# Regrouping a state-space mixer's input and output through DRAM instead of with TensorE transposes

## The chip, the cores and the metric

The kernel runs on one core of a Trainium2 chip. The metric is the device time of one execution in microseconds (us). The engines are called PE (TensorE; PEld is its weight load), DVE (VectorE), ACT (ScalarE), POOL (GpSimd) and SP (SyncE, which only issues DMAs here).

## The reference

A decoder trunk of two layers works on 512 tokens of width 1024, all in float32. In each layer the input is RMS-normalised, one projection makes ten slices of 512 columns, four mixers run on them, each result is multiplied by `silu` of its gate slice, and the output projection is added to the residual. The part that matters here is mixer A, the diagonal complex state-space mixer, run on the slice `u`:

```
h    = rms_norm(x, norm_g);  proj = h @ w_in           # (512, 5120), ten slices of 512
u    = proj[:, 0:512] as (512 tokens, 32 groups, 16)
bu   = einsum('lgh,gph->lgp', u, bbar)                 # complex, 64 states per group
x_l  = abar * x_{l-1} + bu_l                           # scan over the tokens
y    = Re(einsum('lgp,ghp->lgh', x, c)) + d * u
y    = gelu(y.reshape(512, 512))
ga, gb = split(y @ w_glu, 2);  y_a = ga * sigmoid(gb)
mixed = concat(y_a*silu(a_g), y_b*silu(b_g), y_c*silu(c_g), y_m*silu(m_g))
x    = x + mixed @ w_out
```

The other mixers are differential attention (q, k, v), a gated linear recurrence after a width-4 convolution (`cx`; "lru" in the code), and attention into 256 memory tokens.

## The kernel before, in words

Every large product is made of three float32r matmuls: operands are split into a high part and a remainder (`whi`, `wlo` for weights, `hThi`, `hTlo` for the transposed activations). Weights arrive in pieces of 128x1024 (SP's queue), ACT makes `whi` (L166), DVE makes `wlo` (L172), and `w_use` asks for the split of the piece that lies two ahead of the one it hands out. A piece feeds 24 matmuls with 512 moving columns.

`ORDER` lists the projection blocks in the order in which they are run. A block is either token-major (`tm_block`, L537: the activations are the loaded operand and the weights move, result = tokens on partitions) or column-major (`cm_block`, L517: the weights are loaded and the activations move, result = columns on partitions). A block of 512 columns yields eight times, once every 12 matmuls; each yield is a tick. At every tick a small planner (`Streams`) lets each live side stream issue its next portion, and a stream says how many ticks it wants to wait (`D_S5`, `D_AT`, `D_MEM`). So the side streams (attention, lru, memory attention, state-space) are interleaved with the projection matmuls on all engines. `st.join("s5")` ahead of `gl`, the GLU block, issues ticks without projection work until the state-space stream is done.

The state-space stream `s5` works on `U`: partition = (group parity, position within a chunk of four tokens, channel), then 16 group pairs, then 128 chunks. Before the change `u` comes from a token-major block whose loaded operand is `hT` read with a step of four elements (`h_au`), is copied to `au` (L924), and 16 PE transposes with four ACT copies turn it into `U` (L934, L935), one portion of four at each of four ticks. Then, for f = 0 to 3: `states(f)` multiplies `U` by `WT` into the one PSUM tile of tag `sc` (L1004); `turned`, `scans`, `turned_back` are DVE work; `w_rows` and `c_weights` build the weights on DVE, `w_turn` transposes them on PE; `kernel_rows` writes `MT` with eight POOL DMAs (L982); `outputs(f-1)` multiplies `U` by `MT` and `xp` by `VV` (L1010, L1012) with `U` and `xp` as the loaded operands, and ACT copies the result into `yg` (L1014). At the end 16 more PE transposes (L1095) turn `yg`, ACT applies GELU out of PSUM (L1097), and ACT and DVE split the result into `yhi` and `ylo` for `gl`.

Tiles come from pools with a fixed number of buffers: `b8` has 14 of 8 KB, `b2` has ten of 2 KB, PSUM tag `tp` has two banks (shared by all transposes, `outputs`, lru and the memory attention), `sc` one tile of two banks (shared by `states` and the scores of both attentions).

Of the kernel before, what the change touches and what calls it, by code (L numbers as in the profile page):

```python
# [27 lines left out]
ROPE_THETA = 500000.0  # L28


ORDER = ["q v k kv cx au cg bg mq ag mg gl oAM0 oAM1 oBC0 oBC1".split(),
         "q k cx v kv au mq bg mg ag cg gl oAM0 oAM1 oBC0 oBC1".split()]

C_ID, C_DM, C_IF, C_KEEP, C_CM, C_END = 0, 128, 144, 152, 152, 280

# [55 lines left out]
def tile_kernel(ctx: ExitStack, tc: tile.TileContext, A, out):  # L91
# [127 lines left out]
    for l in range(DEPTH):  # L219
        for n in ORDER[l]:  # L220
            if n == "kv":
                for u in range(2):
                    add(l, "mk", u, cm_pieces(A["w_mem_kv"][l], 256 * u))
                add(l, "mv", 0, tm_pieces(A["w_mem_kv"][l], 512))
            elif n == "gl":
                w = A["s5_w_glu"][l].rearrange("(k p) (s c) -> p k s c", p=P, s=2)
                for u in range(2):
                    add(l, "gl", u, [w[:, 2 * i:2 * i + 2, :, 256 * u:256 * u + 256] for i in range(2)])
            elif n[0] == "o":
                ps_ = []  # L230
                for g in n[1:3]:
                    r0 = 512 * "ABCM".index(g)
                    ps_ += tm_pieces(w_out[l, r0:r0 + 512], 512 * int(n[3]))
                add(l, "o", n[1:], ps_)
            elif n in ("q", "k", "v", "au"):
                add(l, n, 0, tm_pieces(w_in[l], COL[n]))
            else:
                for u in range(2):
                    add(l, n, u, cm_pieces(w_in[l], COL[n] + 256 * u))
# [253 lines left out]
    mrs = const.tile([P, 2], F32, tag="mrs", name="mrs")  # L493

    WT = [const.tile([P, 4, 2, 64], F32, tag=f"WT{i}", name=f"WT{i}") for i in range(2)]
    VV = [const.tile([P, 4, 2, T, 16], F32, tag=f"VV{i}", name=f"VV{i}") for i in range(2)]
    MT = const.tile([P, 2, T, 4, 16], F32, tag="MT", name="MT")
    for t_ in WT + VV + [MT]:
        G.memset(t_, 0.0)

# [67 lines left out]
    def h_au():  # L568
        hi = [a.rearrange("p k (c s) -> p k s c", s=T) for a in cur["hi"]]
        lo = [a.rearrange("p k (c s) -> p k s c", s=T) for a in cur["lo"]]  # L570
        return ((lambda k, t: hi[k // 4][:, k % 4, t, :]), (lambda k, t: lo[k // 4][:, k % 4, t, :]))
# [269 lines left out]
    def s5_load(l, R):  # L841
# [7 lines left out]
            nc.sync.dma_start(out=Cw[:, :, i], in_=A[n][l].rearrange("(b g) h p -> (g h) b p", b=4))  # L849
        R["B"], R["Cw"] = B, Cw  # L850

    bbx = const.tile([P, 32, 16], F32, tag="bbx", name="bbx")
    cs_ = const.tile([P, 32, 16], F32, tag="cs_", name="cs_")
    cc_ = const.tile([P, 2, 16, 16], F32, tag="cc_", name="cc_")
# [64 lines left out]
                cn, sn_ = c2, s2  # L919
                yield  # L920

    def au_evac(au):
        def f(s, a):
            S.copy(au[:, :, :, T - 1 - s, :].rearrange("p q g h -> p (q g) h"), a.rearrange("p (a h) -> p a h", h=16))  # L924
        return f

    def s5(l, R):
        au = R["au"]
        U = b8([P, 16, NC], "U")
        for f in range(4):  # L930
            pt = tp()
            for j in range(4):
                q = 4 * f + j
                PE.transpose(pt[:, j, :], au[:, q].rearrange("p g r h -> p (g r h)"), ident)  # L934
            S.copy(U[:, 4 * f:4 * f + 4, :], pt)  # L935
            yield
        yg = b8([P, T, 16, 2, 16], "yg")
        xp = [b2([P, 4, NC], f"xp{i}") for i in range(2)]
        for i in range(2):
            V.memset(xp[i][:, :, 0], 0.0)  # L940
# [36 lines left out]
        def kernel_rows(kq):  # L977

            for t in range(T):
                n = 16 * (t + 1)  # L980
                for g in range(2):
                    G.dma_start(out=MT[g * 64 + 64 - n:g * 64 + 64, g, t], in_=kq[g * 64:g * 64 + n])  # L982

        def c_weights(f):
            qs = slice(4 * f, 4 * f + 4)
            sh = [P, 4, T, 16]
            t1 = b2(sh, "wt1")
            t2 = b2(sh, "wt2")
            a_r = bc(apr[:, l, qs, 1:5], 3, sh)
            a_i = bc(api[:, l, qs, 1:5], 3, sh)  # L990
            c_r = bc(cc_[:, 0, qs], 2, sh)
            c_i = bc(cc_[:, 1, qs], 2, sh)
            for dst, x1, x2, op in ((VV[0], a_r, a_i, ALU.add), (VV[1], a_i, a_r, ALU.subtract)):
                tt(t1, x1, c_r, ALU.mult)
                tt(t2, x2, c_i, ALU.mult)
                for g in range(2):
                    hs = slice(g * 64, (g + 1) * 64)
                    tt(dst[hs, :, g], t1[hs], t2[hs], op)

        def states(f):  # L1000
            B = sc2((P, 2, 4, NC))
# [4 lines left out]

        def outputs(f):
            y = tp()
            for j in range(4):
                PE.matmul(y[:, j, :], U[:, 4 * f + j, :], MT[:, :, :, j, :], start=True, stop=False)  # L1010
                for i in range(2):
                    PE.matmul(y[:, j, :], xp[i][:, j, :], VV[i][:, j].rearrange("p g t h -> p (g t h)"),  # L1012
                              start=False, stop=(i == 1))
            S.copy(yg[:, :, 4 * f:4 * f + 4].rearrange("p t q g h -> p t (q g) h"),  # L1014
                   y.rearrange("p q (g t h) -> p t (q g) h", g=2, t=T))

        def turned(f, B):

# [43 lines left out]
        yield D_S5[0]  # L1062
        kq = w_turn(0, wd)
        yield D_S5[1]
        for f in range(4):
            B = states(f)
            if f:
                outputs(f - 1)
            kernel_rows(kq)
            x_ = turned(f, B)  # L1070
            yield D_S5[2]
            scans(f, x_[0])
            if f < 3:
# [12 lines left out]
        outputs(3)
        yield

        yhi = b8([P, 4, L], "yhi", F32R)
        ylo = b8([P, 4, L], "ylo", F32R)  # L1090
        ygf = yg.rearrange("p t q g h -> p t (q g h)")
        for c in range(4):
            pt = tp()
            for t in range(T):
                PE.transpose(pt[:, t, :], ygf[:, t, c * 128:(c + 1) * 128], ident)  # L1095
            yf = b2([P, NC, T], "yf")
            S.activation(yf.rearrange("p c t -> p t c"), pt, AF.Gelu_apprx_tanh)  # L1097
            yff = yf.rearrange("p c t -> p (c t)")
            S.copy(yhi[:, c, :], yff)
            tt(ylo[:, c, :], yff, yhi[:, c, :], ALU.subtract)  # L1100
            if c == 3:
                S.activation(ti(1, "sq0"), yff[:, 0:1], AF.Exp)
# [52 lines left out]
    for pi, (l, n, u, ids) in enumerate(plan):  # L1155
# [219 lines left out]
```

## Time and profile before

| | |
|---|---|
| time, median of 3 runs | 914.33 us (914.29 to 915.61) |
| profiled execution, its own time | 913.18 us |
| its span | 911.4 us, mean granted TensorE clock 0.998 |
| busy PE / PEld / DVE / ACT / POOL | 890.5 / 748.9 / 658.8 / 509.6 / 42.1 us |
| matmul instructions | 4542 |
| moved by DMA | 90.07 MB, 99 GB/s over the span |

The time is that of the whole execution; the span runs from the first to the last instruction of the profiled one. Matmuls overlap in the pipeline, so the durations of single matmuls sum to more than PE's busy time, and what a matmul costs is the distance from its start to the next one's.

### The profile page before, as it was taken

The page shows a single profiled execution, that of the slowest core. Times are in us where ns is not written, and L with a number is a line of the kernel's source. Part 1 is how long each engine was busy: PE and PEld are TensorE (multiplying, and loading weights), DVE is VectorE, ACT ScalarE, POOL GpSimd, SP SyncE. Part 2 cuts the span into 40 slices and gives each one's busy share as a digit, 9 for nine tenths or more (in the row PEclk, how much of TensorE's full clock was granted, in tenths as well). Part 3 has the DMA queues.
Part 4 walks back from the last instruction along what each step waited for, and adds up shares of the span by engine and source line. Part 5 has one row for each costly group of instructions (what it writes and reads, how often), then busy time and mean ns, then how long its engine had stood idle before and what let it go on. Part 6 is the DMA issues. An engine that isn't in the chain of part 4 may idle for free.

```text
span 911.4 us, 12490 instructions
## 1 busy us (share of the span) xinstructions
PE 890.5 (98%) x4542; PEld 748.9 (82%) x4542; DVE 658.8 (72%) x1315; ACT 509.6 (56%) x1031; POOL 42.1 (5%) x86
## 2 busy tenths in 40 slices
PE   8999999999999999999999999999999999999996
PEld 5788888978878888888888888898888888788885
DVE  6985888678999856983474667764899996666343
ACT  6764887985434265922554568766655344863133
POOL 1001000001110100000100000000101110000000
PEclk9999999999999999999999999999999999999999
DMA  5733432212222237432343332432112222152322
GB/s 185 196 118 102 140 93 70 70 47 72 75 70 61 75 104 205 135 111 93 127 140 92 93 93 70 137 95 70 51 47 83 63 74 93 47 185 98 108 72 93
DMA packets 80930, 90.07 MB, mean 99 GB/s; under 512 B 23778, under 2 KB 58211, under 8 KB 80868
## 3 DMA queue, kind: packets, MB, share of 16 engines
q1 hardware_dynamic: 77842, 85.72, 30.3%
q10 hardware_dynamic: 722, 2.36, 0.8%
q0 software_dynamic: 2304, 1.18, 0.5%
q8 instruction: 36, 0.59, 0.3%
q14 instruction: 26, 0.21, 0.1%
HBM read 84.40 MB, written 4.19 MB: 97 GB/s over the span
## 4 chain that ended last, share of the span: by engine, by line
PE 72%; DVE 18%; ACT 6%; issue 2%; DMA 1%; SPq 0%; DVEq 0%; ACTq 0%
PE acc L537 37%; PE acc L517 17%; PE acc L1261 5%; DVE wlo L172 2%; DVE u L347 2%; DVE xr L1046 2%; DVE wt L347 2%; PE ms L682 1%; DVE xr L347 1%; PE tp L312 1%; PE sc L810 1%; PE tp L1012 1%; PE sc L647 1%; PE sc L648 1%; ACT whi L166 1%
## 5 line engine op out<-in xcount | busy, mean ns | idle before, releaser
L172 DVE TENSOR_TENSOR wlo<-raw,whi 128x1024 fp32r<-128x1024 f32 x136 | 166.2, 1222 | 125.3 <-ACT whi L166 121.6
L166 ACT CAST whi<-raw 128x1024 fp32r<-128x1024 f32 x136 | 143.1, 1052 | 194.1 <-PE acc L537 120.1
L517 PE MATMUL acc<-hThi,whi 128*128 128x512 f32 x384 | 154.3, 402 | 0.0
L517 PE MATMUL acc<-hThi,wlo 128*128 128x512 f32 x384 | 151.1, 394 | 0.0
L517 PE MATMUL acc<-hTlo,whi 128*128 128x512 f32 x384 | 150.6, 392 | 0.0
L537 PE MATMUL acc<-whi,hThi 128*128 128x512 f32 x256 | 104.1, 407 | 1.0 <-ACT whi L166 1.0
L537 PE MATMUL acc<-wlo,hThi 128*128 128x512 f32 x256 | 100.7, 393 | 0.0
L537 PE MATMUL acc<-whi,hTlo 128*128 128x512 f32 x256 | 100.7, 394 | 0.0
L537 PE MATMUL acc<-wlo,mxh 128*128 128x512 f32 x256 | 100.2, 391 | 0.0
L537 PE MATMUL acc<-whi,mxh 128*128 128x512 f32 x256 | 100.1, 391 | 0.0
L537 PE MATMUL acc<-whi,mxl 128*128 128x512 f32 x256 | 100.1, 391 | 0.0
L517 PEld LDWEIGHTS acc<-hThi,wlo 128*128 128x128 f32 x384 | 72.2, 188 | 15.0
L517 PEld LDWEIGHTS acc<-hTlo,whi 128*128 128x128 f32 x384 | 72.4, 189 | 13.4
L517 PEld LDWEIGHTS acc<-hThi,whi 128*128 128x128 f32 x384 | 72.4, 189 | 13.0
L537 PEld LDWEIGHTS acc<-whi,hThi 128*128 128x128 f32 x256 | 56.3, 220 | 9.1 <-ACT whi L166 1.4
L537 PEld LDWEIGHTS acc<-whi,hTlo 128*128 128x128 f32 x256 | 56.1, 219 | 7.8 <-DVE hTlo L315 0.2
L537 PEld LDWEIGHTS acc<-wlo,hThi 128*128 128x128 f32 x256 | 56.4, 220 | 7.1
L537 PEld LDWEIGHTS acc<-whi,mxl 128*128 128x128 f32 x256 | 48.1, 188 | 9.8
L537 PEld LDWEIGHTS acc<-wlo,mxh 128*128 128x128 f32 x256 | 48.1, 188 | 9.7
L537 PEld LDWEIGHTS acc<-whi,mxh 128*128 128x128 f32 x256 | 48.1, 188 | 9.6
L982 POOL DMA_DIRECT2D MT<-kq x64 | 32.1, 509 | 490.7 <-DVE kq L347 339.4
L658 ACT ACTIVATE e<-sc,nmx 128x128 f32<-128x128 f32 (+3 forms) x64 | 33.1, 524 | 7.1 <-DVE nmx L654 5.8
(316 smaller groups left out, 1642.2 us busy)
## 6 DMA issues: line engine op xcount, KB each, us to landing
raw<-in_w_in_dram SPq DMA_DIRECT2D x80, 512.0 KB, 3.7
raw<-in_w_out_dram SPq DMA_DIRECT2D x32, 512.0 KB, 3.3
raw<-in_w_mem_kv_dram SPq DMA_DIRECT2D x16, 512.0 KB, 3.3
x<-in_x_dram SPq DMA_DIRECT2D x8, 512.0 KB, 4.7
raw<-in_s_w_glu_dram SPq DMA_DIRECT2D x16, 256.0 KB, 3.1
mt<-in_mem_dram SPq DMA_DIRECT2D x4, 512.0 KB
xd<-x SPq DMA_DIRECT2D x4, 512.0 KB, 4.0
x<-xd SPq DMA_DIRECT2D x4, 512.0 KB, 5.6
```

Source lines behind the costliest of these rows:

```text
L166: S.copy(hi, wbuf[j])
L172: V.tensor_tensor(out=lo, in0=raw, in1=hi, op=ALU.subtract)
L312: lastins["pe"] = PE.transpose(pt[:, k, :], h[:, kk * 128:(kk + 1) * 128], ident)
L347: V.tensor_tensor(out=o, in0=a, in1=b, op=op)
L517: PE.matmul(a[j][:, :ncol], w[:, kk, c], h(k), start=(hf == 0 and i == 0), stop=(hf == 1 and i == 3 * nh - 1))
L537: PE.matmul(a[t], h(k, t), w[:, kk, :], start=(p == 0 and kk == 0 and i == 0), stop=(p == np_ - 1 and kk == 1 and i == 2))
L647: PE.matmul(s[:, m, :M], qh[:, m, h, :], kT[m][:, h, :M], start=True, stop=False)
L648: PE.matmul(s[:, m, :M], ql[:, m, h, :], kT[m][:, h, :M], start=False, stop=False)
L658: S.activation(e[:, m, :N], s[:, m, :N], AF.Exp, bias=nmx[:, m:m + 1], scale=0.125, accum_out=sm[:, m:m + 1])
L982: G.dma_start(out=MT[g * 64 + 64 - n:g * 64 + 64, g, t], in_=kq[g * 64:g * 64 + n])
L1046: V.tensor_tensor_scan(out=xr_[i][:, j, :], data0=dec, data1=xr_[i][:, j, :], initial=0.0, op0=ALU.mult, op1=ALU.add)
L1261: PE.matmul(a, w[:, k, s, j * 128:(j + 1) * 128], h[:, 2 * hf + k, :], start=(hf == 0 and i == 0), stop=(hf == 1 and i == 5))
```

## The change

`au` becomes a column-major block, so `u` arrives with its columns on partitions. `au_evac` copies each 128 columns to SBUF with the four positions of a chunk apart, and POOL stores them in DRAM (`aud`, four DMAs of 256 KB). The stream `s5` opens with eight POOL DMAs that read `aud` back as `U` (16 partitions each, runs of 512 bytes), and then waits `D_U` = 4 ticks. `outputs` swaps its operands: `MT` and `VV` are loaded and `U` and `xp` move, so the result has (position, group parity, channel) on partitions; ACT copies it to `ys`, four POOL DMAs store it in DRAM (`yd`), and one reads it back as `yl` with all the channels of 128 columns on partitions. GELU then runs on `yl` out of SBUF, some ticks later, in the same loop over f. `MT` and `VV` change their layouts; the `MT` writes have runs of 64 bytes instead of 256. In `ORDER`, `au` moves ahead of `cx` in both layers, and in layer 1 `cx` moves behind `v` and `kv` too. All 32 U transposes and all 32 y transposes of the two layers go.

```diff
-ORDER = ["q v k kv cx au cg bg mq ag mg gl oAM0 oAM1 oBC0 oBC1".split(),
-         "q k cx v kv au mq bg mg ag cg gl oAM0 oAM1 oBC0 oBC1".split()]
+ORDER = ["q v k kv au cx cg bg mq ag mg gl oAM0 oAM1 oBC0 oBC1".split(),
+         "q k v kv au cx mq bg mg ag cg gl oAM0 oAM1 oBC0 oBC1".split()]
...
+D_U = 4
...
-            elif n in ("q", "k", "v", "au"):
+            elif n in ("q", "k", "v"):
                 add(l, n, 0, tm_pieces(w_in[l], COL[n]))
...
-    VV = [const.tile([P, 4, 2, T, 16], F32, tag=f"VV{i}", name=f"VV{i}") for i in range(2)]
-    MT = const.tile([P, 2, T, 4, 16], F32, tag="MT", name="MT")
+    VV = [const.tile([P, 4, T, 2, 16], F32, tag=f"VV{i}", name=f"VV{i}") for i in range(2)]
+    MT = const.tile([P, 4, T, 2, 16], F32, tag="MT", name="MT")
...
-    def au_evac(au):
-        def f(s, a):
-            S.copy(au[:, :, :, T - 1 - s, :].rearrange("p q g h -> p (q g) h"), a.rearrange("p (a h) -> p a h", h=16))
+    def au_evac(R, u):
+        def f(j, a):
+            c = 2 * u + j
+            ac = R["au"][:, c]
+            S.copy(ac, a.rearrange("p (c r) -> p r c", r=T))
+            G.dma_start(out=R["aud"][c * P:(c + 1) * P], in_=ac)
         return f
...
-        for f in range(4):
-            pt = tp()
-            for j in range(4):
-                q = 4 * f + j
-                PE.transpose(pt[:, j, :], au[:, q].rearrange("p g r h -> p (g r h)"), ident)
-            S.copy(U[:, 4 * f:4 * f + 4, :], pt)
-            yield
-        yg = b8([P, T, 16, 2, 16], "yg")
+        src = R["aud"].rearrange("(q g h) s c -> g s h q c", q=16, g=2)
+        for g in range(2):
+            for r in range(T):
+                k = g * 64 + r * 16
+                G.dma_start(out=U[k:k + 16], in_=src[g, T - 1 - r])
+        yf = b8([P, 4, NC, T], "yf")
+        yield D_U
...
-                    G.dma_start(out=MT[g * 64 + 64 - n:g * 64 + 64, g, t], in_=kq[g * 64:g * 64 + n])
+                    G.dma_start(out=MT[g * 64 + 64 - n:g * 64 + 64, :, t, g], in_=kq[g * 64:g * 64 + n])
...
             for j in range(4):
-                PE.matmul(y[:, j, :], U[:, 4 * f + j, :], MT[:, :, :, j, :], start=True, stop=False)
+                PE.matmul(y[:, j, :], MT[:, j].rearrange("p t g h -> p (t g h)"), U[:, 4 * f + j, :], start=True, stop=False)
                 for i in range(2):
-                    PE.matmul(y[:, j, :], xp[i][:, j, :], VV[i][:, j].rearrange("p g t h -> p (g t h)"),
+                    PE.matmul(y[:, j, :], VV[i][:, j].rearrange("p t g h -> p (t g h)"), xp[i][:, j, :],
                               start=False, stop=(i == 1))
-            S.copy(yg[:, :, 4 * f:4 * f + 4].rearrange("p t q g h -> p t (q g) h"),
-                   y.rearrange("p q (g t h) -> p t (q g) h", g=2, t=T))
+            ys = b2([P, 4, NC], "ys")
+            S.copy(ys, y)
+            yd = s5dram.tile([4, 32, T, NC], F32, tag="yd", name=nm("yd"))
+            for t in range(T):
+                G.dma_start(out=yd[:, :, t].rearrange("j k c -> k j c"), in_=ys[32 * t:32 * t + 32])
+            yl = b2([P, T, NC], "yl")
+            G.dma_start(out=yl, in_=yd.rearrange("j k t c -> (j k) t c"))
+            return yl
+
+        def gelu(f, yl):
+            S.activation(yf[:, f].rearrange("p c t -> p t c"), yl, AF.Gelu_apprx_tanh)
+            if f == 3:
+                S.activation(ti(1, "sq0"), yf[:, f, 0, 0:1], AF.Exp)
...
             if f:
-                outputs(f - 1)
+                yl = outputs(f - 1)
...
+            if f:
+                gelu(f - 1, yl)
             yield D_S5[4]
...
-        outputs(3)
-        yield
+        yl = outputs(3)
...
-        for c in range(4):
-            pt = tp()
-            for t in range(T):
-                PE.transpose(pt[:, t, :], ygf[:, t, c * 128:(c + 1) * 128], ident)
-            yf = b2([P, NC, T], "yf")
-            S.activation(yf.rearrange("p c t -> p t c"), pt, AF.Gelu_apprx_tanh)
-            yff = yf.rearrange("p c t -> p (c t)")
...
+        for f in range(4):
+            if f == 3:
+                yield
+                gelu(3, yl)
+            yff = yf[:, f].rearrange("p c t -> p (c t)")
...
-            run(tm_block(h_au(), au_evac(R["au"]), ids))
+            run(cm_block(h_cm(), 8, au_evac(R, u), ids))
```

## Rows read from the trace of the kernel before

**Rows 1.** The page: busy share of an engine, and the chain that ended last by engine.
```profile
PE 890.5 (98%) x4542; PEld 748.9 (82%) x4542; DVE 658.8 (72%) x1315; ACT 509.6 (56%) x1031; POOL 42.1 (5%) x86
...
PE 72%; DVE 18%; ACT 6%; issue 2%; DMA 1%; SPq 0%; DVEq 0%; ACTq 0%
```

**Rows 2.** Engine busy time in four stretches: length, PE, PEld, DVE, ACT, POOL.
```profile
183.40:215.20 31.80, 30.44 (x171) 24.94 (x171) 23.79 (x39) 22.75 (x45) 2.29 (x5) 1.00 0.21 64
215.20:310.50 95.30, 93.12 (x505) 79.14 (x503) 94.25 (x182) 37.78 (x75) 13.76 (x28) 1.00 0.22 66
622.20:656.10 33.90, 33.77 (x187) 27.76 (x185) 22.37 (x40) 22.61 (x54) 4.04 (x8) 1.00 0.21 66
656.10:776.50 120.40, 119.59 (x662) 101.91 (x662) 110.10 (x209) 57.19 (x129) 12.01 (x24) 1.00 0.22 68
```

**Rows 3.** PE in order of time around U transposes: start, duration, line.
```profile
186.43 0.39 PE L647 MATMUL sc<-kT,qh 128*128 128x512 f32 x1
...
188.80 0.60 PE L934 MATMUL tp<-cst,au 128*128 128x128 f32 x4
...
192.01 0.60 PE L934 MATMUL tp<-cst,au 128*128 128x128 f32 x4
192.36 0.48 PE L517 MATMUL acc<-hThi,whi 128*128 128x512 f32 x1
192.68 0.39 PE L517 MATMUL acc<-hTlo,whi 128*128 128x512 f32 x1
...
198.49 0.39 PE L517 MATMUL acc<-hThi,whi 128*128 128x512 f32 x1
...
200.78 0.39 PE L517 MATMUL acc<-hTlo,whi 128*128 128x512 f32 x1
```

**Rows 4.** The transposes ahead of GELU, both layers, as a group of PE.
```profile
L1095 PE MATMUL tp<-cst,yg 128*128 128x128 f32 x32 | 5.0, 274 | 0.1
```

**Rows 5.** PE in the `au` block of layer 0, in order of time.
```profile
173.16 0.40 PE L537 MATMUL acc<-wlo,hThi 128*128 128x512 f32 x1
...
178.33 0.39 PE L537 MATMUL acc<-whi,hTlo 128*128 128x512 f32 x1
```

**Rows 6.** Weight loads by form, 147 to 183.4 us (`au`).
```profile
L537 PEld LDWEIGHTS acc<-wlo,hThi 128*128 128x128 f32 x32 | 10.0, 313 | 0.1
```

**Rows 7.** The same, 40 to 63 us (`v`).
```profile
L537 PEld LDWEIGHTS acc<-wlo,hThi 128*128 128x128 f32 x32 | 6.0, 188 | 1.2
```

**Rows 8.** PEld in order of time, end of layer 1's stream; in brackets its wait.
```profile
782.46 0.42 PEld L828 LDWEIGHTS tp<-cst,me 128*128 128x128 f32 x4 [0.54 <-ACT yf L1097]
...
787.10 1.23 PEld L835 LDWEIGHTS tp<-mpT,kv 128*128 128x128 f32 x6 [0.83 <-ACT yf L1097]
```

**Rows 9.** DVE groups, 110 to 215 us (lru and its convolution).
```profile
L1187 DVE SCALAR_TENSOR_TENSOR xc<-cx,pv,xc 128x509 f32<-128x509 f32 (+2 forms) x12 | 9.0, 749 | 0.2
...
L760 DVE TENSOR_TENSOR_SCAN li<-lr,xc 128x512 f32<-128x512 f32 x4 | 4.9, 1213 | 0.0
...
L747 DVE SCALAR_TENSOR_TENSOR xc<-li,xc 128x512 f32<-128x512 f32 x4 | 2.8, 690 | 0.1
```

**Rows 10.** DVE groups, 183.4 to 334.5 us (last attention items).
```profile
L652 DVE TENSOR_REDUCE mx<-sc 128x2 f32<-128x1024 f32 x2 | 2.4, 1221 | 0.5 <-PE sc L650 0.5
...
L664 DVE SCALAR_TENSOR_TENSOR e<-e,cc 128x512 f32<-128x512 f32 x3 | 2.2, 748 | 0.1
```

**Rows 11.** DMA issues: bytes of each, median us from issue to landing.
```profile
xd<-x SPq DMA_DIRECT2D x4, 512.0 KB, 4.0
...
bd<-in_lru_w_x_dram POOLq DMA_DIRECT2D x4, 64.0 KB, 3.2
...
MT<-kq POOLq DMA_DIRECT2D x16, 16.0 KB, 2.6
```

**Rows 12.** POOL in order of time.
```profile
271.07 4.03 POOL L982 DMA_DIRECT2D MT<-kq  x8 [25.10 <-PE tp L1010]
...
434.44 1.23 POOL L1133 DMA_DIRECT2D bd<-in_lru_w_x_dram  x2
```

More of the change, by code (lines that the diff above doesn't have):

```diff
@@ L566, in h_tm @@
                 (lambda k, t: lo[k // 4][:, k % 4, t * 128:(t + 1) * 128]))
[L568 to L571, printed above, removed]
     def qk_evac(dst):
@@ L850, in s5_load @@
         R["B"], R["Cw"] = B, Cw
+    s5dram = ctx.enter_context(tc.tile_pool(name="s5dram", bufs=2, space=bass.MemoryType.DRAM))
     bbx = const.tile([P, 32, 16], F32, tag="bbx", name="bbx")
@@ L920, in s5_params @@
                 yield
-    def au_evac(au):
-        def f(s, a):
-            S.copy(au[:, :, :, T - 1 - s, :].rearrange("p q g h -> p (q g) h"), a.rearrange("p (a h) -> p a h", h=16))
+    def au_evac(R, u):
[4 more added lines that the diff above has]
+            G.dma_start(out=R["aud"][c * P:(c + 1) * P], in_=ac)
         return f
     def s5(l, R):
-        au = R["au"]
         U = b8([P, 16, NC], "U")
-        for f in range(4):
-            pt = tp()
-            for j in range(4):
-                q = 4 * f + j
-                PE.transpose(pt[:, j, :], au[:, q].rearrange("p g r h -> p (g r h)"), ident)
-            S.copy(U[:, 4 * f:4 * f + 4, :], pt)
-            yield
-        yg = b8([P, T, 16, 2, 16], "yg")
+        src = R["aud"].rearrange("(q g h) s c -> g s h q c", q=16, g=2)
[5 more added lines that the diff above has]
+        yield D_U
         xp = [b2([P, 4, NC], f"xp{i}") for i in range(2)]
@@ L997, in c_weights @@
                     hs = slice(g * 64, (g + 1) * 64)
-                    tt(dst[hs, :, g], t1[hs], t2[hs], op)
+                    tt(dst[hs, :, :, g], t1[hs], t2[hs], op)
         def states(f):
@@ L1064, in s5 @@
         yield D_S5[1]
+        yl = None
         for f in range(4):
@@ L1085, in s5 @@
                 yield D_S5[5]
-        outputs(3)
-        yield
+        yl = outputs(3)
         yhi = b8([P, 4, L], "yhi", F32R)
         ylo = b8([P, 4, L], "ylo", F32R)
-        ygf = yg.rearrange("p t q g h -> p t (q g h)")
-        for c in range(4):
-            pt = tp()
-            for t in range(T):
-                PE.transpose(pt[:, t, :], ygf[:, t, c * 128:(c + 1) * 128], ident)
-            yf = b2([P, NC, T], "yf")
-            S.activation(yf.rearrange("p c t -> p t c"), pt, AF.Gelu_apprx_tanh)
-            yff = yf.rearrange("p c t -> p (c t)")
[L1099 to L1102, printed above, removed]
+        for f in range(4):
[3 more added lines that the diff above has]
+            yff = yf[:, f].rearrange("p c t -> p (c t)")
+            S.copy(yhi[:, f, :], yff)
+            tt(ylo[:, f, :], yff, yhi[:, f, :], ALU.subtract)
             yield
@@ L1192, in tile_kernel @@
         elif n == "au":
-            R["au"] = b8([P, 16, 2, T, 16], "au")
-            run(tm_block(h_au(), au_evac(R["au"]), ids))
+            if u == 0:
+                R["au"] = b8([P, 4, T, NC], "au")
+                R["aud"] = s5dram.tile([GW, T, NC], F32, tag="aud", name=nm("aud"))
+            run(cm_block(h_cm(), 8, au_evac(R, u), ids))
+            if u == 0:
+                continue
             def s5_all(l=l, R=R):
```

## The prediction

> **What bounds the kernel now.** I read the busy shares and the chain first [rows 1]: PE is busy 98% of the span and holds 72% of the chain, DVE 18%. So a microsecond of PE work is worth about a microsecond, unless another engine is full where it is taken away. That is why I next asked for busy time by stretch around the state-space stream [rows 2]. The reader is to see two things there. From `states(0)` to the last `outputs` of layer 0 (215.2 to 310.5 us) PE and DVE are both full: DVE works 94.25 of 95.30 us. In layer 1 the same stretch (656.1 to 776.5) has DVE at 110.10 of 120.40. Ahead of it, from the end of the `au` block to `states(0)`, DVE has room: 23.79 of 31.80 and 22.37 of 33.90 us. The stretches themselves are fixed by ticks, not by the data.
>
> **What it removes on PE.** Transposes come in groups of four. From the start of one such group to the next matmul is 0.35 us (192.01 to 192.36), and that matmul then takes 0.32 us until its successor (192.36 to 192.68), where a plain step is 0.229 us (198.49 to 200.78 are ten) [rows 3]. A group costs 0.35 + 0.09 = 0.44 us. The 32 transposes of the outputs [rows 4] and as many of `U` are 16 groups: 16 x 0.44 = 7.1 us; at least 16 x 0.35 = 5.6 us, where a group stands behind other small matmuls and the slow step would be paid anyway.
>
> The `au` block reads its loaded operand with a step of four elements. Its weight loads take 313 ns [rows 6] against 188 in an ordinary block [rows 7], and its matmuls step by 0.235 us (173.16 to 178.33 are 22 steps) [rows 5] against 0.229: 0.006 x 96 x 2 layers = 1.2 us. Behind each group of small matmuls a long load has nothing to hide under, which I estimate at as much again, so 2 us (bounds 1 and 2.5).
>
> Waits that go with the removed work: at the end of layer 1's stream the memory attention's transposes wait for GELU to free one of the two `tp` banks, 0.54 and 0.83 us in the two longest rows [rows 8]. GELU no longer reads PSUM, so I count 1.5 us for these and their smaller neighbours (0 to 2). Together PE loses 7.1 + 2 + 1.5 = 10.6 us (6.6 to 11.6).
>
> **What costs PE nothing.** `outputs` keeps its 24 matmul instructions of 128 columns for each f; which operand is loaded and which moves does not alter their number, and both sides are 128x128. A strided `MT` becomes a contiguous one, which can only help. ACT loses eight copies of `U`; its GELUs stay.
>
> **The round trip of u.** After the last `au` copy: one POOL store of 256 KB, for which the nearest rows are 4.0 us (512 KB) and 3.2 us (64 KB) [rows 11]; then eight loads, which POOL issues at 1.23/2 = 0.62 us each, the price of the `bd` loads with as many runs [rows 12]; then a last landing of 3.2 us, or 4.0 taken from the larger one. That is 0.6 + 0.6 + 4.0 + 8 x 0.62 + 4.0 = 14 us. Four ticks of `D_U` take the place of the four ticks of transposes, so `states(0)` still stands seven ticks behind the block: 31.80 and 33.90 us [rows 2]. The trip is hidden with some 18 us to spare; without that cover it would cost 14 us per layer. What queues behind its wait on POOL is only `kernel_rows` of f = 0, which `outputs(0)` needs seven ticks after `states(0)`.
>
> **The round trip of y.** ACT copy 0.6, four stores 4 x 0.62 + 3.2, one load 0.62 + 4.0: 11 us. GELU stands at least four ticks of 12 x 0.229 = 2.75 us behind [rows 3], 11 us with nothing else on PE, and more in fact. If `yl` is late by a little, ACT waits with `whi` casts and gate `tanh`s behind it; `whi` is made two pieces (11 us) ahead, so this is free up to some microseconds. Behind the `yl` load on POOL stand the eight `MT` writes, 4.03 us [rows 12], with seven ticks to spare. SP's queue gets no new DMA.
>
> **What moves.** `s5` starts eight ticks earlier relative to `gl`, so its end, three ticks ahead of `gl` now, has eleven. But it now runs into work that used to lie ahead of it, on the engine that is full. In layer 0 three more attention items fall inside the stretch: on DVE 1.22 + 0.75 us [rows 10] and some 0.6 of small instructions each, 7.7 us; on PE 2.37 us each (186.43 to 188.80) [rows 3], 7.1 us. In both layers the whole lru stream falls inside: on DVE four scans of 1.21 and 16 instructions of about 0.69, and half of the twelve convolution steps of 0.75 [rows 9], 4.9 + 11 + 4.5 = 20.4 us; on PE 24 matmuls, 5.6 us. So in layer 0 DVE gets 28 us more (some 25, as records overlap by a tenth), PE 12.7: DVE falls 12 us behind. Splits are ordered two pieces ahead, 2 x 24 x 0.229 = 11 us, and this lead takes most of it; I leave 2 to 3 us of stalls. In layer 1 three heads of the memory attention move out behind the stretch, and DVE was only 91% full, but its first half gets lru all the same: 1 to 2 us. Crowding: 4 us. Its bounds are 0, if the lead and the looser end take it all, and 2 x 12 = 24 us, if nothing does.
>
> **The sum.** Against the profiled execution's 913.18 us (its span is 911.4): 913.18 - 10.6 + 4 = 906.6 us. The median of the runs is 1.15 us above that execution, so 907.7 in their terms; I say 907.5.
>
> **One rule weighed.** Rows first: POOL's `MT` writes are issued at 4.03/8 = 0.50 us each inside a stretch in which DVE is 98.9% busy, and land in 2.6 us [rows 2, 11, 12]. The Trainium skill, page "SBUF — State Buffer", section "SBUF: two separate sides", says that a DMA from the GpSimd queue has its descriptors written by GpSimd, which VectorE locks out while it runs an operation in a two-port mode; its example goes from about 620 to 3100 ns. By that page the eight `U` loads of a layer would take an estimated 20 us more, of which the cover takes 18, and the sum would be some 4 us higher; by the row, nothing. The row decides: these DVE operations do not seem to do it.
>
> **The rivals.**
> *DVE is the new bound (slower).* For it: 94.25 of 95.30 us, and some 25 us more put in. Against it: in the 30 us before the stretch DVE has 8 to 11 us idle, and the lead of the splits. It decides once stalls exceed the 10.6 us gained; with half to all of the 12 us per layer unabsorbed beyond what I counted, 916 to 928 us. The ten `b2` buffers work in the same direction: `turned` holds five, `xp` two, `w_rows` two, and `yl` is now the tenth.
> *The gain is swallowed (same).* Crowding of 9 to 12 us: 913 to 916 us.
> *The round trip of u is late (slower).* If POOL's loads went one at a time, 8 x (0.62 + 4.0) = 37 us and 5 us of store against 32 to 34 us of cover: PE waits some 10 us per layer, 914.3 - 10.6 + 4 + 20 = 928 us. The rows on `MT` speak against it.
> *No crowding at all (faster still).* 914.3 - 10.6 = 903.7 us, or 902 to 903 if lru's departure also eases the start of layer 1.
>
> **How the numbers follow.** Forecast with moderate crowding (904.5 to 912.4): 0.45. No crowding: 0.17. Gain swallowed: 0.14. DVE the bound: 0.19. Late round trip: 0.05. What a measurement of this kernel can tell from no change is about 0.2%, 1.8 us: faster means below 912.5. So faster 0.62, same 0.14, slower 0.24. The range 902 to 920 leaves out about 0.08 below and 0.12 above: the late trip and the worse half of a full DVE. If the change makes the kernel faster, I expect 902 to 912.
>
> **What would show it.** Right: 64 transpose matmuls fewer; `au` weight loads at 188 ns; PE busy down by about 9 us; `states(0)` in both layers without a DMA as the releaser of its wait; GELU rows out of SBUF with no wait over 2 us for `yl`; DVE at 98% or more from `states(0)` on, in layer 1 too, and PE waits on DVE rows (`wlo`, `wt`, `xp`, score maxima) of 2 to 6 us more in sum. Wrong: PE waits of over 10 us in the two stretches with DVE or a pool's buffer as the releaser; `wlo` landing behind its first matmul; a DMA row in front of `states(0)`; more than the present number of ACT table loads around GELU, since it now runs between attention's and lru's exponentials.

## The result and the profile after

The changed kernel takes 956.29 us (median, 953.28 to 959.39), the kernel before on the same chip 914.67 (914.29 to 915.61): a ratio of 1.0454, with a 95% interval of 1.0413 to 1.0494. It is slower by 42 us, where 907.5 us, with 902 to 920 as the range, had been forecast.

The page of the kernel after, its engine line and its chain, answers [rows 1]:

```profile
PE 900.1 (94%) x4478; PEld 744.1 (78%) x4478; DVE 658.1 (69%) x1315; ACT 515.5 (54%) x1029; POOL 81.3 (8%) x150
...
PE 64%; DVE 18%; issue 7%; ACT 7%; DMA 3%; POOL 1%; DVEq 0%; ACTq 0%; POOLq 0%; SPq 0%
```

The 64 transposes are gone (x4478 against x4542), yet PE is busy for longer, and its share of a span of 956.5 us fell from 98 to 94%. The same four figures per stretch as in [rows 2], now for the two stretches from the first `states` matmul of a layer to its last `outputs` (in layer 0 ended, as in [rows 2], some microseconds before that one is through), and for two short ones:

```profile
181.10:321.90 140.80, 123.53 (x630) 100.15 (x630) 121.16 (x221) 74.24 (x134) 21.66 (x39) 0.96 0.22 66
647.40:789.10 141.70, 125.53 (x640) 105.21 (x639) 121.77 (x220) 71.33 (x125) 21.74 (x40) 0.93 0.21 62
...
229.00:236.10 7.10, 7.10 (x50) 6.47 (x49) 0.00 (x0) 3.56 (x8) 4.42 (x9) 1.00 0.19 35
...
246.70:250.00 3.30, 3.30 (x8) 2.62 (x9) 3.30 (x9) 2.91 (x5) 0.00 (x0) 0.53 0.00 0
```

DVE's work in layer 0's stretch rose from 94.25 us to 121.16, by 26.9, as counted ahead (taken to the last matmul of `outputs`, from 100.42 to 126.41, by 26.0). But the stretch is now 140.80 us long, so DVE also stands idle for 19.6 us in it (1.05 before), 7.1 of them in one piece: for 10.6 us its splits (`wlo`) wait for ACT's `whi`, and ACT there waits for PE. What PE waits for (total, times, longest):

```profile
PE acc L518 <- DVE cg L716: 8.8, 2, 8.7
PE tp L960 <- DVE wt L348: 8.1, 3, 5.9
PE acc L518 <- DVE bg L716: 7.8, 2, 4.8
PE acc L518 <- DVE ag L716: 6.3, 2, 3.5
```

Before, `wt` stood in this list with 0.5 us, and no second step of a gate (there L720) at all. Three are of one kind: a matmul block needs one of the four `acc` banks, and a gate's second step on DVE (L716) has not emptied it. The longest, in PE's order of time:

```profile
237.57 0.39 PE L518 MATMUL acc<-hThi,wlo 128*128 128x512 f32 x1
246.61 0.79 PE L518 MATMUL acc<-hThi,whi 128*128 128x512 f32 x1 [8.65 <-DVE cg L716]
247.20 0.63 PE L518 MATMUL acc<-hTlo,whi 128*128 128x512 f32 x1
...
249.76 0.43 PE L518 MATMUL acc<-hTlo,whi 128*128 128x512 f32 x1
250.03 0.40 PE L518 MATMUL acc<-hThi,wlo 128*128 128x512 f32 x1
```

The bank that is missing at 237.6 us had its last matmul at 205.7. Why it was not emptied stands on ACT, whose tanh (L715) comes first:

```profile
235.05 1.05 ACT L167 CAST whi<-raw 128x1024 fp32r<-128x1024 f32 x1 [1.95 <-PE acc L518]
237.77 1.05 ACT L167 CAST whi<-raw 128x1024 fp32r<-128x1024 f32 x1 [1.67 <-PE acc L518]
238.83 1.28 ACT L1024 ACT_TABLE_LOAD   x1
241.90 1.13 ACT L1024 ACTIVATE yf<-yl 128x512 f32<-128x512 f32 x1 [1.79 <-DMA yl<-yd]
242.83 0.63 ACT L749 ACTIVATE a<-lr 128x512 f32<-128x512 f32 x1
243.36 0.58 ACT L715 ACTIVATE th<-acc 128x512 f32<-128x512 f32 x1
```

ACT was often idle between 205.7 and 243.4 us, so it is the instruction's place in its queue that is late. Two readings offer themselves here: it stands behind a GELU that waits for `yl`, or it could get no buffer for `th`. In the built program's list of ACT instructions (not the trace) this tanh is one of two among 32 that wait on semaphores of POOL's DMAs (`DMASW`), although none of them reads a DMA's data:

```
L715 ACTIVATE th_2487<-acc_2354 128x512 [waits DMASW5_49,DMASW6_49,DMASW4_49,Activation_49]
```

Its `b2` buffer is one from which `ys` was being stored. The kernel before has no such tanh. In the trace these waits are over at once (241.9 to 242.0 us), because the tanh stood behind the GELU by then; so this place does not decide between the two readings, and the runs below do.

What came as forecast: `au`'s weight loads run at 188 ns (first row below, 147 to 163 us), and the eight `U` loads are issued by 157.5 us and land in 5.2 us (median), so some 18 us ahead of `states(0)` at 181.1, which waits for nothing.

```profile
L518 PEld LDWEIGHTS acc<-hThi,whi 128*128 128x128 f32 x19 | 3.6, 188 | 0.7
```

```profile
152.97 4.49 POOL L934 DMA_DIRECT2D U<-aud  x8 [2.69 <-DMA aud<-au]
174.69 4.54 POOL L981 DMA_DIRECT2D MT<-kq  x8 [17.23 <-DVE kq L348]
```

POOL issues a `U` load in 4.49/8 = 0.56 us, with DVE busy for 2.28 of the 4.53 us around, and an `MT` write in 0.57, with DVE busy for 4.17 of the 4.54 us. The slowing by DVE for which the Trainium skill ("SBUF — State Buffer", "SBUF: two separate sides") gives an example does not show; the prediction's choice of the row over the page held. Whether any of these DVE operations was of the kind that the page means, no run here shows.

### The profile page after: what moved, and what is told of

Its sections match the earlier page's. It is cut to its first block, busy times and chain, and to the rows that moved or that the text cites. A ratio compares the mean times of both kernels' runs of the same rounds, so it can differ in the third digit from the quotient of the medians.

```text
span 956.5 us, 12468 instructions
## 1 busy us (share of the span) xinstructions
PE 900.1 (94%) x4478; PEld 744.1 (78%) x4478; DVE 658.1 (69%) x1315; ACT 515.5 (54%) x1029; POOL 81.3 (8%) x150
## 4 chain that ended last, share of the span: by engine, by line
PE 64%; DVE 18%; issue 7%; ACT 7%; DMA 3%; POOL 1%; DVEq 0%; ACTq 0%; POOLq 0%; SPq 0%
PE acc L538 31%; PE acc L518 17%; PE acc L1272 5%; DVE wlo L173 2%; DVE u L348 2%; DVE xr L1057 2%; DVE wt L348 1%; PE ms L678 1%; PE tp L313 1%; ACT whi L167 1%; DVE xp L348 1%; DVE xr L348 1%; DMA raw<-in_w_in_dram 1%; PE sc L643 1%; DVE VV L348 1%
## 5 line engine op out<-in xcount | busy, mean ns | idle before, releaser
L518 PE MATMUL acc<-hThi,whi 128*128 128x512 f32 x448 | 182.5, 407 | 25.2 <-DVE cg L716 8.8
L518 PE MATMUL acc<-hThi,wlo 128*128 128x512 f32 x448 | 179.8, 402 | 0.0
L518 PE MATMUL acc<-hTlo,whi 128*128 128x512 f32 x448 | 179.3, 400 | 0.0
L518 PEld LDWEIGHTS acc<-hTlo,whi 128*128 128x128 f32 x448 | 86.6, 193 | 16.8
L538 PE MATMUL acc<-whi,hThi 128*128 128x512 f32 x192 | 77.1, 402 | 0.8 <-ACT whi L167 0.8
L538 PE MATMUL acc<-wlo,hThi 128*128 128x512 f32 x192 | 75.4, 393 | 0.0
L538 PE MATMUL acc<-whi,hTlo 128*128 128x512 f32 x192 | 75.3, 394 | 0.0
L538 PEld LDWEIGHTS acc<-whi,hThi 128*128 128x128 f32 x192 | 36.4, 190 | 8.6 <-ACT whi L167 1.2
L538 PEld LDWEIGHTS acc<-whi,hTlo 128*128 128x128 f32 x192 | 36.2, 189 | 7.6 <-DVE hTlo L316 0.2
L538 PEld LDWEIGHTS acc<-wlo,hThi 128*128 128x128 f32 x192 | 36.3, 189 | 6.9
L654 ACT ACTIVATE e<-sc,nmx 128x128 f32<-128x128 f32 (+3 forms) x64 | 33.2, 525 | 11.1 <-DVE nmx L650 10.7
```

Source lines behind the costliest of these rows:

```text
L518: PE.matmul(a[j][:, :ncol], w[:, kk, c], h(k), start=(hf == 0 and i == 0), stop=(hf == 1 and i == 3 * nh - 1))
L538: PE.matmul(a[t], h(k, t), w[:, kk, :], start=(p == 0 and kk == 0 and i == 0), stop=(p == np_ - 1 and kk == 1 and i == 2))
L654: S.activation(e[:, m, :N], s[:, m, :N], AF.Exp, bias=nmx[:, m:m + 1], scale=0.125, accum_out=sm[:, m:m + 1])
```

## The experiments

Four ideas were set against each other. *Crowding* (or *overlap*): `ORDER` puts lru and attention onto a full DVE. *Buffers*: the ten 2 KB buffers, or the fourteen of 8 KB, run out. *ACT queue*: GELUs inside the loop wait with tanhs behind them. *Place*: `au` ahead of `cx` costs by itself, for instance by tiles held at another time. All times are medians; the kernel before took 914.1 to 914.9 us beside them.

### The two halves of the change apart

Old `ORDER`, u and y through DRAM:

```diff
-ORDER = ["q v k kv au cx cg bg mq ag mg gl ...", "q k v kv au cx mq bg mg ag cg gl ..."]
+ORDER = ["q v k kv cx au cg bg mq ag mg gl ...", "q k cx v kv au mq bg mg ag cg gl ..."]
```

> The changed kernel with the ORDER of before: cx ahead of au again, u and y still through DRAM. Buffer theory (the ten 2 KB buffers do not suffice: lru's four weight tiles, the seven to nine of the state-space stream, and ys and yl, each held over a DMA; a gate's tanh waits for a buffer, its accumulator stays occupied and PE stands): lru's weights are back before the stream takes its buffers, ys and yl still press, 905 to 930 us. Crowding theory (lru and three attention items moved onto a full DVE): all of the loss returns and the transposes' gain remains, 903 to 910 us. ACT-queue theory (GELUs inside the loop wait for yl with tanhs and whi casts behind them, and bring table loads): the GELUs stand as before, 940 us or more.

Measured: 924.55 us, ratio 1.0109 (1.0094 to 1.0124).

The kernel before with the new `ORDER` alone (the same two lines, the other way):

> The kernel before with the ORDER of after alone: transposes, no DRAM, GELUs at the end. Buffer theory: lru's four and the stream's nine are more than ten even without ys and yl, 925 to 945 us. Crowding theory: the whole loss and none of the gain, 950 to 968 us. ACT-queue theory: nothing of it is here, 912 to 918 us.

Measured: 960.85 us, ratio 1.0499 (1.0481 to 1.0517). So `ORDER` alone costs 46 us on the old code and 956.3 - 924.6 = 32 us on the new. And the rest of the change costs 10 us in the old `ORDER`, where it should have gained that much.

The old code, its `ORDER` too, with u alone through DRAM (column-major `au`, `aud`, the eight `U` loads, `D_U`):

> The kernel before, its ORDER too, with u alone through DRAM (column-major au, eight groups of transposes less); y keeps its transposes and the GELUs out of PSUM. By the prediction's terms 8 x 0.44 + 2 = 5.5 us less than before: 908 to 910 us. If the round trip of u is late, 914 us or more.

Measured: 908.52 us, ratio 0.9938 (0.9923 to 0.9953): 5.7 us less, for 5.5 forecast.

### Where ys and yl lie, and where the GELUs stand

New `ORDER`; `ys` and `yl` share one 8 KB tile that replaces `yf`, GELUs at the end into `b2` tiles:

```diff
-        yf = b8([P, 4, NC, T], "yf")
+        yy = b8([P, 4, T, NC], "yy")
...
-            ys = b2([P, 4, NC], "ys")
+            ys = yy[:, f]
...
-            yl = b2([P, T, NC], "yl")
+            yl = yy[:, f]
...
-            if f:
-                gelu(f - 1, yl)
```

> The changed kernel with ys and yl in one 8 KB tile that takes the place of yf, so they use none of the 2 KB buffers, and the GELUs at the end of the stream as before the change (out of SBUF). New ORDER kept. Buffer theory: two of thirteen buffers less are wanted, part of the loss returns, 920 to 940 us. Crowding theory: the order is unchanged, 948 to 960 us. ACT-queue theory: no GELU waits in the loop any more, 905 to 915 us.

Measured: 940.81 us, ratio 1.0286 (1.0269 to 1.0303). The same with the GELUs left in the loop and `yf` kept as one more 8 KB tile:

> As the run before in this list, but the GELUs stay in the loop and write yf, an 8 KB tile beside the one that holds ys and yl. New ORDER kept. Buffer theory: as without the GELUs in the loop, within 8 us of that run, 920 to 945 us. Crowding theory: 948 to 960 us. ACT-queue theory: the GELUs wait and load tables as in the changed kernel, 950 to 960 us.

Measured: 938.95 us, ratio 1.0265 (1.025 to 1.0281). Two of the ten 2 KB buffers less in use are worth 15 to 17 us; where the GELUs stand makes no difference here. In the old `ORDER`, GELUs at the end:

> The ORDER of before, u and y through DRAM, ys and yl in one 8 KB tile instead of two of the 2 KB buffers, GELUs at the end. Buffer theory: the 10 us by which the old ORDER alone was still slower than before came from ys and yl; without them the removed transposes show, 902 to 910 us. Crowding theory: ys and yl never mattered in the old ORDER, 918 to 926 us. A third view, that the round trip of y through DRAM is itself what is late: as crowding, 918 to 926 us, with PE waits on the yl landing or at the end of the stream.

Measured: 903.68 us, ratio 0.988 (0.9864 to 0.9897), faster than both kernels. Its page, and its two stretches as above:

```profile
PE 880.9 (98%) x4478; PEld 732.3 (81%) x4478; DVE 658.3 (73%) x1315; ACT 511.5 (57%) x1027; POOL 81.2 (9%) x150
```

```profile
219.00:316.40 97.40, 95.52 (x524) 80.98 (x523) 96.38 (x184) 38.76 (x75) 22.17 (x40) 1.00 0.30 84
651.50:774.70 123.20, 122.39 (x688) 104.73 (x688) 110.95 (x209) 66.61 (x138) 21.65 (x39) 1.00 0.27 80
```

PE lost 890.5 - 880.9 = 9.6 us of busy time and waits for less than 1 us at a time in the stretches, although DVE works 96.38 of its 97.40 us. With the GELUs in the loop and `yf` as one 8 KB tile more, in the old `ORDER`:

> The ORDER of before, ys and yl in one 8 KB tile, and the GELUs inside the loop with yf as one more 8 KB tile: against the changed kernel with the old ORDER only the place of ys and yl differs, against the version with the GELUs at the end only the GELUs. Buffer theory (with the old ORDER the 21 us between those two are the two 2 KB buffers that wait for DMAs): 902 to 910 us. ACT-queue theory (they are the GELUs in the loop, which wait for yl with tanhs behind them): 918 to 926 us.

Measured: 918.6 us, ratio 1.004 (1.0027 to 1.0054). That looked like the ACT queue, but all 15 us are at one place in layer 1 (PE waits, then DVE in order of time):

```profile
PE sc L806 <- ACT me L814: 10.2, 2, 6.7
```

```profile
759.30 1.22 DVE L808 TENSOR_REDUCE mmx<-sc 128x4 f32<-128x1024 f32 x1 [2.81 <-PE sc L806]
...
765.56 1.28 DVE L716 SCALAR_TENSOR_TENSOR ag<-th,acc 128x512 f32<-128x512 f32 x2 [2.60 <-PE sc L806]
```

`ag`'s first write waits for PE's scores of the memory attention, which it does not read, and with the banks held, PE has only these heads to do, one after the other. That points to `ag`'s own 8 KB buffer: in the built program it is the one of `qm`, the queries that these scores read (in the next run it is `qT`'s). A GELU in place in `yy`, still in the loop, tells it from the GELUs (`yhi` and `ylo` then read `yy` with a stride):

```diff
-            S.activation(yf[:, f].rearrange("p c t -> p t c"), yl, AF.Gelu_apprx_tanh)
+            S.activation(yl, yl, AF.Gelu_apprx_tanh)
```

> Old ORDER, GELUs inside the loop, each in place in the one 8 KB tile that ys and yl use, so one 8 KB tile less than the version of 918.6 us while the stream runs; the split into yhi and ylo reads with a stride. If the 15 us above 903.7 are the 8 KB tile: 902 to 907 us. If they are the GELUs in the loop, with their waits for yl and their table loads: 915 to 921 us.

Measured: 904.47 us, ratio 0.9894 (0.988 to 0.9909). The 15 us were the 8 KB tile. The GELUs do wait in the loop, and nobody minds; ACT's row:

```profile
ACT yy L1024 <- DMA yy<-yd: 5.6, 4, 3.2
```

And since this run and the first of all have the same `ORDER` and the GELUs at the same place, 924.55 - 904.47 = 20 us are the two 2 KB buffers. Two more runs put `ys` and `yl` into the `au` tile, new `ORDER` with GELUs at the end, and old `ORDER` with GELUs in the loop:

> New ORDER, GELUs at the end, ys and yl in the au tile, which is dead by then: one 8 KB tile less than the version of 940.8 us. If the 8 KB buffers hold up the gates (bg's first write in layer 1 stood behind lru's last scan): 922 to 932 us. If DVE is simply full: within 4 us of 940.8.

> Old ORDER, GELUs in the loop, ys and yl in the dead au tile: one 8 KB tile less than the version of 918.6 us, as many as the version of 903.7 us. If the 15 us between those two are the 8 KB tile: 902 to 908 us. If they are the GELUs in the loop: 915 to 921 us.

Measured: 945.62 us, ratio 1.0338 (1.032 to 1.0356), and 929.18, ratio 1.0154 (1.0139 to 1.0169). The expectation had miscounted: `au` otherwise goes back to its pool before the stream begins, so the stream had no tile less. They show only that keeping `au` for this costs 5 to 11 us.

### More buffers in the changed kernel

SBUF has no room for one more buffer. Two `whi` and two `wlo` tiles instead of three set 8 KB free (control), which then go to the big or to the small buffers:

```diff
-    NRAW, NHI, NLO = 2, 3, 3
+    NRAW, NHI, NLO = 2, 2, 2
...
-    big = ctx.enter_context(tc.tile_pool(name="big", bufs=14))
+    big = ctx.enter_context(tc.tile_pool(name="big", bufs=15))
```

> Control for the next two: the changed kernel with two whi and two wlo tiles instead of three, so each piece is split one piece ahead instead of two. It sets 8 KB free and uses none of it. Any theory: slower than the changed kernel by what the lead is worth, 960 to 990 us.

> The control with the 8 KB as a fifteenth big (8 KB) buffer. Buffer theory in the form that the big buffers are short (a gate's tile waits for lru's last read): 10 to 25 us below the control. Crowding theory: within 4 us of the control.

> The control with the 8 KB as four more 2 KB buffers, fourteen instead of ten. Buffer theory in the form that the 2 KB buffers are short: 12 to 30 us below the control. Crowding theory: within 4 us of the control.

Measured: control 968.56 us, ratio 1.0592 (1.0576 to 1.0608); fifteen big buffers 968.78, ratio 1.0595 (1.058 to 1.0611); fourteen small ones 960.9, ratio 1.0508 (1.0492 to 1.0524). With this lead a fifteenth 8 KB buffer returns nothing; four more 2 KB buffers return 8 us, less than expected and far less than `ORDER` costs.

### The overlap that the new ORDER makes

In the version of 940.8 us, `ys` and `yl` are out of the way. Its DVE work in the two stretches, and what PE waits for:

```profile
182.63:315.94 133.31, 118.41 (x620) 96.43 (x619) 121.17 (x222) 68.82 (x128) 21.64 (x39) 0.96 0.21 62
642.50:770.20 127.70, 112.67 (x610) 93.98 (x609) 118.98 (x218) 66.32 (x120) 21.67 (x40) 0.93 0.22 65
```

```profile
PE acc L518 <- DVE bg L716: 15.4, 2, 13.6
PE acc L518 <- DVE wlo L173: 11.1, 4, 6.7
```

The 11.1 us are all in layer 0: splits that come late. The 13.6 us are one stall in layer 1 (PE, then DVE):

```profile
727.63 0.79 PE L518 MATMUL acc<-hThi,whi 128*128 128x512 f32 x1 [13.56 <-DVE bg L716]
```

```profile
725.17 1.22 DVE L756 TENSOR_TENSOR_SCAN li<-lr,xc 128x512 f32<-128x512 f32 x1
726.30 0.67 DVE L348 TENSOR_TENSOR xr<-xr,u 128x512 f32<-128x512 f32 x1
726.89 1.28 DVE L716 SCALAR_TENSOR_TENSOR bg<-th,acc 128x512 f32<-128x512 f32 x2
```

`bg`'s first step stands behind lru's last scan, and in the built program `bg`'s 8 KB tile lies in the buffer of `xc`, which that scan reads. DVE works all through the stall. The kernel before with the new `ORDER` has the same stall, of 13.6 us too, ending at 734.0. So a held 8 KB buffer takes part in the cost of `ORDER`; how much of it is the buffer and how much a full DVE is not separated. With fifteen 8 KB buffers `bg` lies in `v`'s buffer instead of `xc`'s, and in that kernel nothing came back.

The same version with the stream held back by eight more ticks:

```diff
-D_U = 4
+D_U = 12
```

> The new ORDER with ys and yl in one 8 KB tile and the GELUs at the end (940.8 us), and the stream of the state-space part held back by eight more ticks (12 instead of 4), so that its states, lru's steps and the gates stand to each other as in the old ORDER. Overlap theory (the cost of the ORDER is that lru and attention items fall into the same ticks as the stream): 902 to 912 us. Place theory (the cost is au ahead of cx itself, for instance the four weight tiles and the big tiles of lru held at another time): 930 to 945 us.

Measured: 921.56 us, ratio 1.0083 (1.0065 to 1.01): half of the 37 us between 940.8 and 903.7, and in neither forecast. The expectation had the distance wrong. In layer 0, lru starts 15 ticks ahead of `states(0)` in the old `ORDER`, 1 behind it in the new one, and 7 ahead of it here: half of the distance, half of the cost. The distance is not all that changed, though: `bg` of layer 1 lies in `v`'s buffer here, and its stall is gone. What is left, in layer 0 (DVE between 241 and 267 us; then PE):

```profile
241.00:267.00 26.00, 19.43 (x98) 15.80 (x97) 25.91 (x44) 5.35 (x9) 7.23 (x13) 0.95 0.22 65
```

```profile
267.04 0.80 PE L518 MATMUL acc<-hThi,wlo 128*128 128x512 f32 x1 [5.87 <-DVE wlo L173]
```

DVE works 25.91 of 26.00 us on the stream, lru's tail, splits and gates, and the split `wlo` comes 5.9 us late: the stall that the prediction had described. Sixteen ticks restore the distance (with `ys` and `yl` in `au`, so against 945.6 us):

> As the first of this list with the stream held back by sixteen more ticks (20 instead of 4): lru then stands to the states as in the old ORDER, but the stream eight ticks later against the gates and against the GLU block, so up to five ticks without projection work stand ahead of that. Overlap theory: 904 to 916 us. If place or buffers of lru are the cost: 922 us or more.

Measured: 945.22 us, ratio 1.0312 (1.0278 to 1.0346), a miss in the total. Starts of four landmarks in layer 0, read from each trace as the n-th matmul into `acc` (625th, 1057th, 1105th, and the first of layer 1):

| | before | after | 903.7 us version | 940.8 us version | 20 ticks |
|---|---|---|---|---|---|
| `cg` begins | 183.7 | 180.0 | 185.5 | 181.5 | 180.3 |
| second half of `mg` | 323.0 | 346.5 | 321.0 | 341.4 | 318.5 |
| `gl` begins | 334.5 | 357.4 | 331.9 | 352.3 | 343.6 |
| layer 1 begins | 461.7 | 483.2 | 459.2 | 478.1 | 475.7 |

Up to the second half of `mg` the 20 ticks take the whole loss back (318.5 us), though the stream, through at 316.6 us in the 903.7 us version, has until 348.5 to go here. The loss returns behind that, where the stream ends late: in the same run PE waits 6.2 us for the memory attention's `mpT` and 6.2 for the GLU's `yhi`.

```profile
PE tp L831 <- DVE mpT L348: 6.2, 1, 6.2
PE acc L1271 <- ACT yhi L1107: 6.2, 2, 4.4
```

Holding lru back instead, by 20 ticks:

```diff
+        yield 20
         bd = R["bd"]
```

> The same version with the new ORDER and 4 ticks, and lru instead held back by 20 ticks, so that most of it stands behind the stream's first half; its four weight tiles stay occupied for as long. If lru's overlap is most of the cost: 905 to 922 us. If it is the stream's earlier place against attention and the gates, or the buffers that lru holds: 930 to 950 us.

Measured: 976.67 us, ratio 1.0683 (1.0666 to 1.0699), worse than anything else, with one stall of some 16 us in each layer:

```profile
PE acc L518 <- DVE ag L716: 31.6, 2, 15.8
```

In the built program, `ag`'s first write waits for six (layer 0) and seven (layer 1) of POOL's DMA semaphores, and reads no DMA's data. Its tile lies in the buffer of the stream's `yy` in both layers: lru keeps its own tiles for longer, and `ag` gets an 8 KB buffer only when the stream gives one back. That was not tried further.

### DVE's work by itself

The 940.8 us version without 16 of lru's DVE instructions a layer (12 of 0.69 us and four scans of 1.21, [rows 9]: 13 us):

```diff
-            V.scalar_tensor_tensor(out=xc[:, c, :], in0=i_[:, c, :], scalar=1.0, in1=xc[:, c, :], ...)
...
-            V.scalar_tensor_tensor(out=i_[:, c, :], in0=a2, scalar=1.0, in1=i_[:, c, :], ...)
...
-            tt(xc[:, c, :], xc[:, c, :], i_[:, c, :], ALU.mult)
-            V.tensor_tensor_scan(out=i_[:, c, :], data0=r_[:, c, :], data1=xc[:, c, :], ...)
```

> The version of 940.8 us (new ORDER, 4 ticks) with lru's DVE steps behind the first phase left out: two products, the square-root factor's product and the scan, 16 instructions and some 14 us of DVE work a layer (lru's result is not computed). Its ACT and PE work and its buffers stay. If DVE's fullness is the cost: 908 to 922 us. If buffers or the chain of waits through ACT and PE are: 930 to 941 us.

Measured: 924.97 us, ratio 1.0104 (1.0087 to 1.0121): 16 us less, between the two forecasts. DVE's busy time fell from 658.1 to 634.8 us, by 23.3 (the records overlap), so 0.68 us came back for a microsecond. Not all of it is DVE's work: `bg` of layer 1 lies in `v`'s buffer in this program, and PE waits 1.5 us there instead of 13.6. The 903.7 us version with 28 more DVE instructions a layer:

```diff
             x_ = turned(f, B)
+            for _ in range(7):
+                tt(x_[1], x_[2], x_[3], ALU.mult)
```

> The version of 903.7 us (old ORDER, GELUs at the end) with seven more DVE instructions of 128x512 (about 0.69 us each) behind each turned, 28 a layer, 19 us of DVE work a layer in the stream's stretch; what they write is overwritten. If a full DVE in that stretch is enough to cost what the new ORDER costs: 930 us or more. If the cover (the splits' lead, DVE's idle time ahead of the stretch) takes such work, and the new ORDER costs by something else: 904 to 915 us.

Measured: 931.33 us, ratio 1.0193 (1.0165 to 1.0221): 28 us, for a busy time of DVE that rose from 658.3 to 691.0 us, by 32.7: 0.85 us a microsecond. No block was moved and no tile added, `bg` keeps its buffer (`kT`'s), and the stalls are of the same kinds:

```profile
PE tp L960 <- DVE wt L348: 6.0, 4, 4.5
PE acc L518 <- DVE wlo L173: 4.3, 1, 4.3
PE acc L518 <- DVE ag L716: 4.1, 3, 2.0
```

So DVE work put into the stretch costs 0.85 us a microsecond with nothing else changed; taken out, it gave 0.68 back.

## Why the prediction was wrong

**The gain was right.** 10.6 us were forecast for the removed work. With what hid it out of the way, 10.7 (914.37 - 903.68) and 9.6 (914.09 - 904.47) were measured, of which u's part is 5.7, for 5.5. How the 10.6 us divide between transposes, weight loads and waits, no run separates. That the swap of operands costs nothing held too: loads and matmuls of `outputs` take 192 and 275 to 276 ns (median) before and after. The round trip of u is hidden with the 18 us to spare that were forecast. That of y is late for ACT, by up to 3.7 us in the changed kernel and 3.2 in the 904.47 us run, which PE does not feel.

**The step that failed first is crowding**, "this lead takes most of it; I leave 2 to 3 us of stalls", so 4 us with 24 as the upper bound. `ORDER` costs 32 us in the changed kernel, 37 with `ys` and `yl` out of the 2 KB buffers, and 46 alone. The work that it moves was counted well in layer 0 (26.9 us measured, some 25 to 28 forecast). Wrong were three things. The two-piece lead does not take the lag: in the version of 940.8 us PE waits 11.1 us for `wlo` in layer 0, nearly all of the 12 us by which DVE was to fall behind. And it protects the splits alone; what fails first in the changed kernel is the emptying of the four `acc` banks, which has no lead of its own and stands in the queues behind the stream, lru and attention. Layer 1 was priced at 1 to 2 us because DVE was 91% full there; its stretch got 121.77 - 110.10 = 11.7 us of DVE work more, and from its first matmul to `gl` layer 1 takes 835.4 - 483.2 = 352.2 us, where the kernel before took 324.3. Of the 37 us, layer 0 has 478.1 - 459.2 = 18.9, and layer 1 about as much, most of it the stall of 13.6 us at `bg`. And each long stall is followed by microseconds at half of PE's clock, which the sum had nothing for. In the version of 940.8 us the stretches hold 121.17 - 96.38 = 24.8 and 118.98 - 110.95 = 8.0 us of DVE work more than in that of 903.7; at 0.68 to 0.85 us a microsecond that is 22 to 28 of the 37 us, an estimate. The rest was not divided among `bg`'s buffer, attention's items, lru's work on ACT and PE, and clock.

**The second is a price that was missing.** `yl` as "the tenth" of the `b2` buffers stood in the text only as something that works in a rival's direction, and the count left out `ys` and the four weight tiles that lru holds in the same pool while it runs. `ys` and `yl` in that pool cost 20 us in the old `ORDER` and 15 to 17 in the new one, enough by themselves to turn a gain of 10 into a loss of 10. Buffers last as long as what reads them, and here that is a DMA: 2.1 us of landing for a store and 3.5 for the load, plus their turns in POOL's queue. The Trainium skill ("Perfetto Trace Analysis", "Optimization Strategy") says that repeating gaps on the engine that should be saturated can mean there is no room for the next tile. Here the gaps were single and irregular (5.0 us for `xp`, 4.0 and 1.9 for `ag` in the 924.55 us run), and it held all the same.

**The signs of being wrong were well named, with one too many.** PE's waits on DVE came to far more than 10 us (the four rows above are 31 us), though none is longer than 8.7. Six table loads at GELU's line instead of one came as well, and 10.2 us of waits for `yl`; they cost nothing that could be found.

**The rival** "DVE is the new bound" named DVE's work and the 2 KB buffers, the two causes found, at 916 to 928 us and a chance of 0.19. Its price took DVE's lag as the ceiling of the loss.

The parts, each the difference of two runs that follow on each other: 914.3 - 9.8 (work removed, GELUs in the loop) + 20.1 (two 2 KB buffers) + 31.7 (`ORDER`) = 956.3 us. Taken in another order they are of other sizes (37 us for `ORDER` and 15 to 17 for the buffers).

## What to carry to other kernels

Where one engine is full beside the bounding one, price work moved onto it at most of its length (0.85 us a microsecond here), not at what is left over after a prefetch lead; and ask which resource that has no lead (here the PSUM banks) is emptied by that engine, and whose buffers its results wait for. A tile that a DMA reads or writes holds its buffer for the whole round trip: count the pool at its fullest moment, and put such tiles where memory is reserved anyway. Judge a change of several parts by its parts: here one gained 10 us, and its buffers and its order lost 52.

## What the runs showed of the hardware

PE's granted clock fell while it stood still and stayed low for some time after. In the 938.95 us run, PE waits from 711.5 to 725.2 us; granted clock (1.00 is 2.4 GHz, 0.50 is 1.2) and PE's instructions in six stretches:

```profile
708.00:711.40 3.40, 2.99 (x24) 2.56 (x23) 3.31 (x6) 1.43 (x3) 0.00 (x0) 1.00 0.00 0
711.50:714.00 2.50, 0.18 (x2) 0.00 (x0) 2.50 (x4) 0.59 (x1) 2.47 (x5) 1.00 0.04 7
714.00:716.00 2.00, 0.00 (x0) 0.00 (x0) 2.00 (x4) 0.00 (x0) 2.00 (x5) 0.64 0.68 141
716.00:725.20 9.20, 0.00 (x0) 0.00 (x0) 9.17 (x15) 3.99 (x5) 2.75 (x5) 0.50 0.27 91
725.30:728.60 3.30, 3.30 (x9) 2.63 (x10) 3.30 (x7) 1.42 (x2) 0.00 (x0) 0.56 0.09 28
728.70:732.00 3.30, 3.30 (x17) 2.71 (x16) 3.30 (x9) 0.00 (x0) 0.00 (x0) 1.00 0.35 123
```

In the first 3.3 us after the stall PE does 9 matmuls, in the next 17. In the changed kernel the same is seen at 246.61 us: a first step of 0.59 us, six of 0.43 until 249.76, and soon 0.23 again. Seven steps take 3.15 us instead of 7 x 0.229 = 1.6, so the 8.65 us stall costs some 1.5 us more than it shows. The mean granted clock of the changed kernel is 0.979, that of the 903.7 us version 0.998; the same 4478 matmuls keep PE busy for 900.1 us in the one and 880.9 in the other.
